# A second feed-forward by seven block products: one change to a two-layer diffusion step on one core

## The chip, the core and the metric

The kernel runs on one core of one Trainium2 chip, as one program. The metric is device time in microseconds (us). Before the change three runs took 1517.56 to 1518.67 us, median 1517.86. Besides these there is one execution recorded by the hardware profiler. A core has five engines that follow one instruction queue each and wait for each other by semaphores: TensorE (PE in the rows; PEld is its loading of weights), VectorE (DVE), ScalarE (ACT), GpSimd (POOL) and SyncE (SP), which here only starts DMA transfers. Matrix products are written to PSUM, everything else lives in SBUF.

## What is computed

The reference is one step of a two-layer network on 128 context tokens and 512 latent tokens of 1024 features. Each layer has a mixer and then a gated feed-forward with a convolution of three taps along the tokens; both are followed by a residual, a layer norm and a modulation by six vectors that come from a conditioning row c. What matters here is the feed-forward, with 2 x 2816 columns in `w_up`:

```python
def _conv_ffn(h, w_up, conv_w, conv_b, w_down):
    z = _dwconv(h @ w_up, conv_w, conv_b, 1, 1)
    g, v = z[..., :D_FF], z[..., D_FF:]
    return (jax.nn.silu(g) * v) @ w_down
...
        xp = _layernorm(ALPHA * xp + g2c * fp, ln2_g[l], ln2_b[l])
        xs = _layernorm(ALPHA * xs + g2s * fs, ln2_g[l], ln2_b[l])
```

The change touches it in layer 1, the second of the two. Everything is in float32.

## The kernel before

**Tokens.** Features lie on the 128 partitions and tokens along the columns: 128 context tokens, two columns of zeros, 512 latent tokens, T = 642 in all. `TOK` (line 26) has the five token tiles of 128.

**Products.** A float32 product is made of three passes of the format fp32r: each operand is split into a rounded part (hi) and what is left (lo), and `mm3` (line 152) adds hi x hi, hi x lo and lo x hi (lines 155, 156 and 157). `split` (line 97) makes the two parts: hi is a cast, mostly on ScalarE (line 99), lo a subtraction (line 102), of the activations on VectorE, of most weights on GpSimd.

**The feed-forward (`ffn`, line 534).** 2816 columns are 22 pairs of 128, each of a gate and a value. For one of the two, `ntile` makes 24 matmuls for the first 258 columns of tokens and 24 for the other 384, into one PSUM tile of 1024 columns (`A`, two of them). `conv` takes it from PSUM: ScalarE the middle tap with the bias (line 557), VectorE the outer taps (lines 558 and 559), ScalarE the Silu of the gate (line 561). `finish` multiplies the two (line 569, VectorE) and splits the product, which waits in the pool `s` for the down projection.

**The down projection.** It runs in parts (`PIECES`, line 28) of 4, 4, 4, 3, 3 and 4 pairs, and part q comes after the second pair of the part behind it. For a part and each of five token tiles there are two groups of matmuls of 512 columns, three to each pair, into a PSUM tile `B` (four of them). `accumulate` adds a group to `y` in SBUF (line 495 on VectorE; line 493 on ScalarE copies the first part's). The last part is added with the layer's gate and goes through the norm to the output.

**Weights.** SyncE's order of transfers is as written: `want` puts a weight tile in a queue, `load` starts its transfer into a raw buffer (`r`, four), `prep` splits it into the pool `w` (12 buffers of 4 KB per partition; a weight tile takes two). In layer 1 the value weight of the first pair and the odd down tiles have their lo made on VectorE, the others on GpSimd.

**Work beside it.** `back` is a list of generators, of which `tick` does one step at a time. In this stretch it holds `lazy` (line 439; the layer norm's factors and offsets applied to y on VectorE, lines 457 and 458) and `mod_vec` (line 257; the sixth modulation vector: VectorE multiplies rows of `wmT` by c, line 250, 16 instructions). c itself, after a Silu (line 1433), lies in the pool `v`, which has two buffers. Ahead of the last part comes `merge` (line 611), whose sums are on GpSimd (line 627).

**What sets the order.** SyncE's instructions stand as written. For the other engines a scheduler orders the instructions when the kernel is built, by when it reckons that they can begin; on the chip each engine then follows its row strictly. The transposes ahead of the first pair (`turn`, line 425, transposes on line 434 of what line 420 made) write the activations as hi and lo tiles of 2 x 642 columns.

## Time and profile before

| | |
|---|---|
| three runs, median | 1517.86 us |
| profiled execution, its own time | 1517.38 us |
| its span, first to last instruction | 1515.6 us |
| TensorE busy, matmuls | 1455.9 us (96%), 8768 |
| VectorE busy | 982.1 us (65%) |
| ScalarE busy | 599.9 us (40%) |
| GpSimd busy | 535.6 us (35%) |
| mean granted TensorE clock | 0.990 |

Shares are of the span. All rows are of the profiled execution; times in them count from the start of its span, and the 1.8 us between span and time lie around it. The shares are averages over stages with different limits, so the stretch that a change touches has to be read by itself: the second feed-forward goes from about 1030 us to the end. In a row, "<-" stands between what is written and what is read; a number in square brackets is how long the engine stood before the instruction, with the one that released it.

### The profile page before, as it was taken

Reading aid. Unit: us, or ns where it says so; the run is one execution under the profiler, and the core shown is the slowest. Engines: PE = TensorE matmul, PEld = TensorE weight load, DVE = VectorE, ACT = ScalarE, POOL = GpSimd, SP = SyncE. Lnnn points to the kernel's source line nnn. Section 1 sums busy time; section 2 is a strip of 40 time slices with the busy share of each in tenths; the row PEclk is TensorE's granted clock in tenths of the full one; section 3 lists DMA queues with packets and bytes.
Section 4 is the critical chain, followed back from the end, with each engine's and each line's share of the span. In section 5 each row is a group of like instructions: output and inputs, shape, how many; then the busy total and the mean of one; then the engine's idle time right before and its main releaser. Section 6 shows DMA issues by size and latency. Waiting matters only on the chain. (4 is left out here: it accounts for less than half of the span.)

```text
span 1515.6 us, 21970 instructions
## 1 busy us (share of the span) xinstructions
PE 1455.9 (96%) x8768; PEld 1311.8 (87%) x8768; DVE 982.1 (65%) x1498; ACT 599.9 (40%) x890; POOL 535.6 (35%) x431
## 2 busy tenths in 40 slices
PE   7989999999999999998999999999999999999997
PEld 5876879989898989888988888778999989898995
DVE  4685688456867697768699577767763424333558
ACT  3422354333132323235686656336333313132223
POOL 2241444333242425453462102853313232232343
PEclk9999999999999999999999999999999999999999
DMA  9544705344454445241321003433444222132231
GB/s 377 222 160 163 278 14 200 107 140 161 159 168 139 157 163 178 87 156 45 120 74 46 1 2 126 169 110 111 139 125 129 82 78 76 43 112 97 74 108 70
DMA packets 54757, 188.10 MB, mean 124 GB/s; under 512 B 6592, under 2 KB 7168, under 8 KB 54656
## 3 DMA queue, kind: packets, MB, share of 16 engines
q1 hardware_dynamic: 54656, 186.71, 36.4%
q8 instruction: 69, 1.13, 0.3%
q14 instruction: 32, 0.26, 0.1%
HBM read 175.96 MB, written 10.72 MB: 123 GB/s over the span
## 5 line engine op out<-in xcount | busy, mean ns | idle before, releaser
L102 POOL TENSOR_TENSOR w<-r,w 128x1024 fp32r<-128x1024 f32 (+2 forms) x130 | 326.3, 2520 | 679.7 <-ACT w L99 664.4
L155 PE MATMUL A<-s,w 128*128 128x258 f32 (+1 forms) x1672 | 524.1, 314 | 13.0 <-DVE t L559 5.9
L156 PE MATMUL A<-s,w 128*128 128x258 f32 (+1 forms) x1672 | 521.9, 312 | 0.5 <-DVE s L102 0.5
L157 PE MATMUL A<-s,w 128*128 128x258 f32 (+1 forms) x1672 | 521.2, 312 | 0.0
L155 PEld LDWEIGHTS A<-s,w 128*128 128x128 f32 x1672 | 317.5, 190 | 24.7 <-issue 14.2
L156 PEld LDWEIGHTS A<-s,w 128*128 128x128 f32 x1672 | 318.1, 190 | 4.3 <-issue 2.5
L99 ACT CAST w<-r 128x1024 fp32r<-128x1024 f32 (+2 forms) x181 | 183.8, 1033 | 345.3 <-PE B L156 136.3
L157 PEld LDWEIGHTS A<-s,w 128*128 128x128 f32 x1672 | 317.9, 190 | 2.5 <-issue 2.5
L155 PE MATMUL B<-w,s 128*128 128x512 f32 (+2 forms) x734 | 282.1, 386 | 3.4 <-DVE y L495 2.0
L156 PE MATMUL B<-w,s 128*128 128x512 f32 (+2 forms) x734 | 281.7, 384 | 2.9 <-DVE w L102 2.9
L157 PE MATMUL B<-w,s 128*128 128x512 f32 (+2 forms) x734 | 280.8, 384 | 0.9 <-DVE s L102 0.9
L558 DVE SCALAR_TENSOR_TENSOR t<-A,vec,t 128x641 f32<-128x641 f32 x88 | 77.7, 883 | 215.5 <-ACT t L557 215.5
L155 PEld LDWEIGHTS B<-w,s 128*128 128x128 f32 x734 | 137.7, 188 | 31.6 <-DVE y L495 2.2
L156 PEld LDWEIGHTS B<-w,s 128*128 128x128 f32 x734 | 137.8, 188 | 30.5 <-DVE w L102 3.7
L157 PEld LDWEIGHTS B<-w,s 128*128 128x128 f32 x734 | 138.0, 188 | 29.2 <-DVE s L102 1.4
L250 DVE SCALAR_TENSOR_TENSOR t<-r,v 128x1024 bf16<-128x1024 f32 x112 | 157.3, 1415 | 4.2 <-DMA r<-in_wmT_dram 3.2
L99 ACT CAST s<-t 128x642 fp32r<-128x642 f32 x60 | 43.8, 730 | 183.7 <-DVE t L569 148.8
L102 DVE TENSOR_TENSOR w<-r,w 128x1024 fp32r<-128x1024 f32 (+3 forms) x51 | 73.1, 1451 | 61.5 <-ACT w L99 61.4
L495 DVE TENSOR_TENSOR y<-B,y 128x512 f32<-128x512 f32 x80 | 54.7, 687 | 62.0 <-PE B L157 61.9
L557 ACT ACTIVATE t<-A,vec 128x642 f32<-128x642 f32 x88 | 77.7, 883 | 14.2 <-PE A L157 14.2
L559 DVE SCALAR_TENSOR_TENSOR t<-A,vec,t 128x641 f32<-128x641 f32 x88 | 77.8, 884 | 2.5
L561 ACT ACTIVATE t<-t 128x642 f32<-128x642 f32 x44 | 32.7, 742 | 99.7 <-DVE t L559 93.9
(259 smaller groups left out, 1596.8 us busy)
## 6 DMA issues: line engine op xcount, KB each, us to landing
r<-in_w_up_dram SPq DMA_DIRECT2D x88, 512.0 KB, 3.7
r<-in_wmT_dram SPq DMA_DIRECT2D x56, 512.0 KB, 3.3
r<-in_w_dn_dram SPq DMA_DIRECT2D x44, 512.0 KB, 4.0
s<-scr SPq DMA_DIRECT2D x20, 512.0 KB, 7.8
s<-in_wm_dram SPq DMA_DIRECT2D x16, 512.0 KB, 9.3
r<-in_wm_dram SPq DMA_DIRECT2D x16, 512.0 KB, 4.6
kept<-y SPq DMA_DIRECT2D x10, 512.0 KB, 3.5
r<-kept SPq DMA_DIRECT2D x10, 512.0 KB, 3.5
```

The source lines that it names most:

```text
L99: act.copy(hi, src)
L102: return lo_eng.tensor_tensor(lo, src, f(hi), ALU.subtract)
L155: pe.matmul(out, ah, bh, start=i == 0, stop=False)
L156: pe.matmul(out, ah, bl, start=False, stop=False)
L157: pe.matmul(out, al, bh, start=False, stop=i == n - 1)
L250: op = dve.scalar_tensor_tensor(junk, raw, 1.0, cb[s], ALU.mult, ALU.mult, accum_out=mc[l][:, m, s, k:k + 1])
L495: dve.tensor_tensor(acc[i][:, sl], ps, acc[i][:, sl], ALU.add)
L557: act.activation(t, z, AF.Identity, bias=cb, scale=w1)
L558: dve.scalar_tensor_tensor(t[:, 1:], z[:, :T - 1], w0, t[:, 1:], ALU.mult, ALU.add)
L559: dve.scalar_tensor_tensor(t[:, :T - 1], z[:, 1:], w2, t[:, :T - 1], ALU.mult, ALU.add)
L561: act.activation(t, t, AF.Silu)
```

## The change

The up projection of layer 1 is computed by blocks (`ffn_w`, which takes the place of `ffn(1, ...)`). The activations h are cut in halves of features (512 each) and halves of tokens (322 and 320 of the 642 columns, overlapping in two columns, so that every block has 322): A11, A12 by features for the first tokens, A21, A22 for the others. A pair's weights are four blocks of 512 x 128: B11 and B21 of the gate, B12 and B22 of the value. In place of the eight products of blocks there are seven, each of a block or a sum of blocks (Winograd's form of Strassen's scheme), and the four results are sums of the seven. Each product is 4 x 3 matmuls of 322 columns. The sums of activations S1 to S4 are made once, on VectorE, by `sums`, between the first pairs; while that goes on, the first `NPLAIN` = 2 pairs are computed as before. The sums of weights are made for each pair on GpSimd (four instructions of 512 columns, in `block`), each of the seven weight blocks is split with its lo on VectorE, and takes one buffer of the pool `w`; the lo of the down tiles is all on GpSimd. The results of the products are added on VectorE (`add`, seven instructions of 322 columns) into SBUF tiles zg and zv, from which the convolution now reads. `free` counts the weight buffers that are given back, and `pump_w` issues the next preparation when there is room among the 12.

The down projection goes in parts of three pairs (the last of four), each right after the pair that follows it. The norm's factor and offset rows lie in the pool `v` instead of `s`, and the rows of c for the sixth modulation are read by the generator `last_gate`, after the norm's rows.

The diff, cut to its core (after the change `split` stands at line 101, with the cast at line 103 and lo at line 106):

```diff
+PARTS = (0, 3, 6, 9, 12, 15, 18, 22)
+NPLAIN = 2
+TH = T // 2 + 1
+T2 = T - TH
...
+    def new_quads():
+        return [[[S([128, 4, TH], F32R) for _ in range(2)] for _ in range(2)] for _ in range(2)]
...
+            if self.quads:
+                cuts = ((c.start, min(c.stop, TH), 0), (max(c.start, T2), c.stop, 1))
+                for a, b, th in cuts:
+                    if a >= b:
+                        continue
+                    for kh in range(2):
+                        d = slice(a - th * T2, b - th * T2)
+                        split(hi[kh][th][:, :, d], lo[kh][th][:, :, d], p4[kh][:, :, a - c.start:b - c.start], act, dve)
+                return
...
-                    t = (S if n == 1 else Tm)([128, w])
+                    t = (Tm if n > 1 else V if self.l else S)([128, w])
...
+    def ffn_w(h):
...
+        ops = {"A11": (hi[0][0], lo[0][0]), "A12": (hi[1][0], lo[1][0]), "A22": (hi[1][1], lo[1][1])}
+        ORDER = ("A11", "S2", "S3", "A12", "S1", "A22", "S4")
...
+        def pump_w():
+            while tasks and live[0] + tasks[0][0] <= 12:
+                c, fn = tasks.pop(0)
+                live[0] += c
+                fn()
+        def free(n):
+            live[0] -= n
+            pump_w()
+        def block(p, j):
+            w = W([128, 2, 512], F32R)
+            wh, wl = w[:, 0, :], w[:, 1, :]
+            if j < 6:
+                g = raw(("g", p))
+                b11, b21 = g[:, :512], g[:, 512:]
+            v = raw(("v", p))
+            b12, b22 = v[:, :512], v[:, 512:]
+            src = b22 if j == 6 else (b11, b11, b12, b21, b12, b21)[j]
+            if j == 1:
+                pool.tensor_tensor(b12, b22, b12, ALU.subtract)
+                pool.tensor_tensor(b11, b12, b11, ALU.add)
+            elif j == 4:
+                pool.tensor_tensor(src, b22, b11, ALU.subtract)
+            elif j == 5:
+                pool.tensor_tensor(src, b21, b11, ALU.subtract)
+            split(wh, wl, src, act, dve)
+            ready_w[("u", p, j)] = w
+            if j == 5:
+                done(("g", p))
+            elif j == 6:
+                done(("v", p))
...
+        def plain(p):
+            r = raw(("d", p))
+            wh, wl = W([128, D], F32R), W([128, D], F32R)
+            split(wh, wl, r, act, pool)
...
+        def plan():
+            for p in range(NPLAIN, NP):
+                loads.append((("g", p), w_up[l, 2 * p]))
+                loads.append((("v", p), w_up[l, 2 * p + 1]))
+                for j in range(7):
+                    tasks.append((1, lambda p=p, j=j: block(p, j)))
+                if p in PARTS[1:]:
+                    q = PARTS.index(p) - 1
+                    yield q
+            yield NW - 1
+        for q in plan():
+            for d in range(PARTS[q], PARTS[q + 1]):
+                loads.append((("d", d), w_dn[l, d]))
+                tasks.append((2, lambda d=d: plain(d)))
...
+        def sums():
+            for n in ("S1", "S2", "S3", "S4"):
+                ops[n] = (S([128, 4, TH], F32R), S([128, 4, TH], F32R))
+            a11, a12, a21, a22 = ops["A11"], ops["A12"], (hi[0][1], lo[0][1]), ops["A22"]
+            for q in range(2):
+                ks = slice(2 * q, 2 * q + 2)
+                def part(pair):
+                    return f(pair[0][:, ks, :]), f(pair[1][:, ks, :])
+                def fin(n, src):
+                    split(ops[n][0][:, ks, :], ops[n][1][:, ks, :], src, act, dve)
+                def pair_op(x, y, op):
+                    t, e = Tm([128, 2, TH]), Tm([128, 2, TH])
+                    dve.tensor_tensor(t, x[0], y[0], op)
+                    dve.tensor_tensor(e, x[1], y[1], op)
+                    dve.tensor_tensor(t, t, e, ALU.add)
+                    return t
+                b11, b12, b21, b22 = (part(z) for z in (a11, a12, a21, a22))
+                s1 = pair_op(b21, b22, ALU.add)
+                fin("S1", s1)
+                yield
+                s2 = Tm([128, 2, TH])
+                dve.tensor_tensor(s2, s1, b11[0], ALU.subtract)
+                dve.tensor_tensor(s2, s2, b11[1], ALU.subtract)
+                fin("S2", s2)
+                yield
+                s4 = Tm([128, 2, TH])
+                dve.tensor_tensor(s4, b12[0], s2, ALU.subtract)
+                dve.tensor_tensor(s4, s4, b12[1], ALU.add)
+                fin("S4", s4)
+                yield
+                s3 = pair_op(b11, b21, ALU.subtract)
+                fin("S3", s3)
...
+        def up(p):
+            c1, c2, e = slice(0, TH), slice(TH, T), slice(TH - T2, TH)
+            p1, zg, zv = Tm([128, TH]), Tm([128, T]), Tm([128, T])
...
+            ps = A()
+            act.copy(p1, product(0, ps, 0))
+            free(1)
+            add(zv[:, c1], product(1, ps, 512), p1)
+            free(1)
+            ps = A()
+            add(zv[:, c2], product(2, ps, 0)[:, e], zv[:, e])
+            free(1)
+            add(zg[:, c1], product(3, ps, 512), p1)
+            free(1)
+            ps = A()
+            x5 = product(4, ps, 0)
+            add(zv[:, c1], x5, zv[:, c1])
+            free(1)
+            add(zg[:, c2], product(5, ps, 512)[:, e], zv[:, c2])
+            add(zv[:, c2], x5[:, e], zv[:, c2])
+            free(1)
+            tg = conv(zg, p, 0)
+            tick()
+            add(zv[:, c1], product(6, B(), 0), zv[:, c1])
+            free(1)
+            tv = conv(zv, p, 1)
+            tick(1 if p < NP - 2 else 3)
+            finish(p, tg, tv)
...
+        def rest(make_norm):
...
+            for p in range(1, NPLAIN):
+                up_plain(p)
+                free(4)
+            for _ in extra:
+                pass
...
+                up(p)
+                if p in PARTS:
+                    q = PARTS.index(p) - 1
+                    down(q)
...
-    nxt = nxt.rest(lambda: Norm(1, 0, (1, SA2)), sub(ffn, 1))
-    cb = [V([128, D]) for _ in range(2)]
-    for s in range(2):
-        sp.dma_start(cb[s], crow[s:s + 1].to_broadcast([128, D]))
-        act.activation(cb[s], cb[s], AF.Silu)
-    back.append(mod_vec(1, (5,), cb))
-    nxt.rest(lambda: Norm(1, 2, None), None)
+    nxt = nxt.rest(lambda: Norm(1, 0, (1, SA2)), sub(ffn_w))
+    def last_gate():
+        cb = [V([128, D]) for _ in range(2)]
+        for s in range(2):
+            sp.dma_start(cb[s], crow[s:s + 1].to_broadcast([128, D]))
+            act.activation(cb[s], cb[s], AF.Silu)
+        yield
+        yield from mod_vec(1, (5,), cb)
+    back.append(last_gate())
+    nxt.rest(lambda: Norm(1, 2))
```

**VectorE behind the second pair.** t and s are the temporaries and sums of `sums`, w weight buffers, y the rows that the norm is applied to. Before:

```order
L558 SCALAR_TENSOR_TENSOR t_9986<-A_9937,vec,t_9986 128x641
L457 TENSOR_TENSOR y_8735<-y_8735,s_9991 128x512
L559 SCALAR_TENSOR_TENSOR t_9986<-A_9937,vec,t_9986 128x641
L458 TENSOR_TENSOR y_8735<-y_8735,s_9993 128x512
L457 TENSOR_TENSOR y_8735<-y_8735,s_9991 128x512
L457 TENSOR_TENSOR y_8737<-y_8737,s_9991 128x512
```

After, from the same convolution on:

```order
L819 SCALAR_TENSOR_TENSOR t_9973<-A_9924,vec,t_9973 128x641
L785 TENSOR_TENSOR t_9986<-s_9399,s_9401 128x644
L820 SCALAR_TENSOR_TENSOR t_9973<-A_9924,vec,t_9973 128x641
L786 TENSOR_TENSOR t_9987<-s_9403,s_9405 128x644
L106 TENSOR_TENSOR w_10067<-r_9914,w_10067 128x512
L787 TENSOR_TENSOR t_9986<-t_9986,t_9987 128x644
L106 TENSOR_TENSOR w_10072<-r_9919,w_10072 128x512
L795 TENSOR_TENSOR t_9993<-t_9986,s_9398 128x644
L106 TENSOR_TENSOR s_9979<-t_9986,s_9978 128x644
L796 TENSOR_TENSOR t_9993<-t_9993,s_9402 128x644
L819 SCALAR_TENSOR_TENSOR t_10047<-A_9998,vec,t_10047 128x641
L106 TENSOR_TENSOR s_9981<-t_9993,s_9980 128x644
```

Between the instructions of two convolutions stand now the sums of halves (644 columns, lines 785 to 796), with their lo halves (s, line 106), where the norm's work (lines 457 and 458) stood, and lo halves of the coming blocks' weights (w, line 106); the norm's instructions stand further on.

**VectorE at the end of a down part.** y is what the parts are added to, B a group of matmuls. Before, at the end of the second part:

```order
L495 TENSOR_TENSOR y_10712<-B_11381,y_10712 128x512
L495 TENSOR_TENSOR y_10712<-B_11395,y_10712 128x512
L495 TENSOR_TENSOR y_10744<-B_11409,y_10744 128x512
L495 TENSOR_TENSOR y_10744<-B_11423,y_10744 128x512
L558 SCALAR_TENSOR_TENSOR t_11504<-A_11455,vec,t_11504 128x641
L559 SCALAR_TENSOR_TENSOR t_11504<-A_11455,vec,t_11504 128x641
```

After, at the end of the fourth part, up to the first sum of a product of the pair behind it (line 872):

```order
L514 TENSOR_TENSOR y_10496<-B_12203,y_10496 128x512
L514 TENSOR_TENSOR y_10524<-B_12214,y_10524 128x512
L106 TENSOR_TENSOR w_12236<-r_12005,w_12236 128x512
L106 TENSOR_TENSOR w_12241<-r_12116,w_12241 128x512
L514 TENSOR_TENSOR y_10524<-B_12225,y_10524 128x512
L106 TENSOR_TENSOR w_12244<-r_12116,w_12244 128x512
L106 TENSOR_TENSOR w_12249<-r_12239,w_12249 128x512
L106 TENSOR_TENSOR w_12252<-r_12116,w_12252 128x512
L106 TENSOR_TENSOR w_12255<-r_12239,w_12255 128x512
L106 TENSOR_TENSOR w_12276<-r_12116,w_12276 128x512
L872 TENSOR_TENSOR t_12261<-A_12262,t_12259 128x322
L106 TENSOR_TENSOR w_12295<-r_12239,w_12295 128x512
```

Where the next convolution followed the last groups, seven lo halves of weight blocks now stand ahead of the next pair's first sum.

**ScalarE and the rows of c.** v is the pool with two buffers. Before, in the odd layer's mixer ahead of the feed-forward:

```order
L389 ACTIVATE y_8735<-y_8735,m_9459,m_9464 128x512 x2
L1433 ACT_TABLE_LOAD
L1433 ACTIVATE v_9921<-v_9921 128x1024
L1433 ACTIVATE v_9922<-v_9922 128x1024
L370 ACTIVATE t_9510,m_9506<-y_8737,m_9505 128x1024
```

After, in the first part of the down projection:

```order
L512 COPY y_10524<-B_10525 128x512
L103 CAST w_10552<-r_10266 128x512
L103 CAST w_10557<-r_10379 128x512
L1750 ACTIVATE v_10437<-v_10437 128x1024
L512 COPY y_10524<-B_10536 128x512
L1750 ACTIVATE v_10438<-v_10438 128x1024
L875 COPY t_10575<-A_10578 128x322
L103 CAST w_10560<-r_10379 128x512
L103 CAST w_10565<-r_10555 128x512
```

The Silu of c moved from ahead of the feed-forward into its first down part, among the copies of that part's groups (line 512), the casts of weight blocks (line 103) and the copy of the next pair's first product (line 875).

## Rows read from the trace of the kernel before

**Rows 1.** Busy time by stretch (view of windows; columns are in the first line).

```profile
core 0: us, PE busy (x) PEld busy (x) DVE busy (x) ACT busy (x) POOL busy (x), PEclk, DMA share, GB/s
1051.19:1065.45 14.26, 14.26 (x96) 14.26 (x97) 10.24 (x11) 7.57 (x9) 6.72 (x3) 1.00 0.58 217
1030.00:1477.00 447.00, 442.83 (x2673) 417.47 (x2672) 213.48 (x274) 145.26 (x179) 135.69 (x65) 1.00 0.32 99
1036.86:1040.26 3.40, 3.40 (x19) 3.40 (x18) 3.40 (x7) 0.37 (x1) 0.76 (x2) 0.53 0.00 0
```

**Rows 2.** What TensorE waited for, 1030 to 1477 us: total, times, longest.

```profile
PE B L434 <- DVE t L420: 2.4, 1, 2.4
```

**Rows 3.** VectorE in order of time inside a down part: start, duration, what.

```profile
1220.24 0.69 DVE L495 TENSOR_TENSOR y<-B,y 128x512 f32<-128x512 f32 x1 [2.10 <-PE B L157]
1223.03 0.69 DVE L495 TENSOR_TENSOR y<-B,y 128x512 f32<-128x512 f32 x1 [2.10 <-PE B L157]
```

**Rows 4.** VectorE's groups, 1100 to 1300 us: total, mean ns, idle before.

```profile
L250 DVE SCALAR_TENSOR_TENSOR t<-r,v 128x1024 bf16<-128x1024 f32 x16 | 19.2, 1221 | 2.1 <-DMA r<-in_wmT_dram 1.9
L559 DVE SCALAR_TENSOR_TENSOR t<-A,vec,t 128x641 f32<-128x641 f32 x20 | 17.7, 886 | 0.7
...
L569 DVE TENSOR_TENSOR t<-t,t 128x642 f32<-128x642 f32 x11 | 9.1, 826 | 0.3
L495 DVE TENSOR_TENSOR y<-B,y 128x512 f32<-128x512 f32 x12 | 8.3, 690 | 17.4 <-PE B L157 17.4
...
L250 DVE DVE_READ_ACCUMULATOR t<-r,v 128x1 f32 x16 | 1.3, 82 | 0.0
```

**Rows 5.** VectorE in order of time, 1040 to 1115 us.

```profile
1054.24 2.49 DVE L569 TENSOR_TENSOR t<-t,t 128x642 f32<-128x642 f32 x1 [0.54 <-ACT t L561]
...
1066.20 1.28 DVE L457 TENSOR_TENSOR y<-y,s 128x512 f32<-128x512 f32 x2
1067.40 0.68 DVE L458 TENSOR_TENSOR y<-y,s 128x512 f32<-128x512 f32 x1
1068.00 0.88 DVE L558 SCALAR_TENSOR_TENSOR t<-A,vec,t 128x641 f32<-128x641 f32 x1
1068.80 2.10 DVE L458 TENSOR_TENSOR y<-y,s 128x512 f32<-128x512 f32 x1
```

**Rows 6.** TensorE in order of time, 1028 to 1066 us.

```profile
1029.77 0.66 PE L434 MATMUL B<-ident,t 128*128 128x128 f32 x4 [0.91 <-POOL t L420]
...
1030.63 0.29 PE L155 MATMUL A<-s,w 128*128 128x258 f32 x1
...
1036.45 0.66 PE L434 MATMUL B<-ident,t 128*128 128x128 f32 x4 [2.39 <-DVE t L420]
...
1038.12 0.42 PE L155 MATMUL A<-s,w 128*128 128x258 f32 x1
```

**Rows 7.** The buffers v from 1000 us: min/median/max ns, starts, shape.

```profile
L1433 ACT ACTIVATE v<-v x2: 1046/1054/1061, 1011.8 to 1012.7; 128x1024 f32<-128x1024 f32 x2
...
DMA to landing us min/median/max: 7.5/7.9/8.3
```

**Rows 8.** ScalarE's casts (line 99), 1030 to 1477 us, by shape.

```profile
L99 ACT CAST w<-r x63: 1030/1051/1057, 1044.4 to 1462.9; 128x1024 fp32r<-128x1024 f32 x63
...
L99 ACT CAST s<-t x21: 729/730/735, 1056.8 to 1469.1; 128x642 fp32r<-128x642 f32 x21
L99 ACT CAST s<-B x12: 350/373/415, 1033.2 to 1044.1; 128x256 fp32r<-128x256 f32 x12
```

**Rows 9.** GpSimd's sums of 512 columns (line 627), whole span.

```profile
L627 POOL TENSOR_TENSOR y<-y,r x20: 1287/1300/1824, 619.2 to 1467.1; 128x512 f32<-128x512 f32 x20
```

**Rows 10.** ScalarE's groups in a pair, 1030 to 1477 us.

```profile
L557 ACT ACTIVATE t<-A,vec 128x642 f32<-128x642 f32 x43 | 37.9, 882 | 3.4 <-PE A L157 3.4
...
L561 ACT ACTIVATE t<-t 128x642 f32<-128x642 f32 x22 | 16.3, 742 | 44.1 <-DVE t L559 44.1
```

**Rows 11.** GpSimd in order of time, about 1053 and 1066 us.

```profile
1053.65 2.40 POOL L102 TENSOR_TENSOR w<-r,w 128x1024 fp32r<-128x1024 f32 x1 [0.56 <-ACT w L99]
...
1066.61 3.73 POOL L102 TENSOR_TENSOR w<-r,w 128x1024 fp32r<-128x1024 f32 x1 [4.69 <-ACT w L99]
```

## What is expected, before the changed kernel was run

> **What bounds the kernel now.** I read the busy times of the stretch that the change touches, then what TensorE waited for in it, then the durations of the other engines' instructions there. In the second feed-forward (1030 to 1477 us) TensorE is busy 442.8 of 447 us, VectorE 213.5 (48%), ScalarE 145.3 and GpSimd 135.7 [rows 1]. Of the 4.2 us in which TensorE stood, 2.4 are one wait at the head of the stretch [rows 2]. So TensorE sets the pace, at full clock: the plain pair from 1051.19 to 1065.45 is 96 matmuls in 14.26 us [rows 1], 0.1485 each. What TensorE is spared is won, unless another engine now comes late. That engine is to be looked for.
>
> **What is saved.** Twenty pairs go from 96 matmuls (48 of 258 columns, 48 of 384, mean 321) to 84 of 322. No row has that width; it lies between the two, so I take 0.149 us: 12.52 a pair, 1.74 saved, 34.8 in all (1 us either way). The order has 240 rows fewer on TensorE, which is 20 x 12, so the change does what it says. The down projection keeps its 660 matmuls. Twelve of them come every 2.79 us [rows 3], so a group of nine takes 2.09 and a part of three (ten groups) 20.9. Against the profiled execution's 1517.4 us (the median of the runs is 0.5 above) that is 1482.6 if nothing waits.
>
> **VectorE's new load.** A pair had four conv instructions of 0.886, a product of 0.826, and a low half of the same width [rows 4], 5.2 us, and at times a weight's low half. All stay (two of the conv inputs now lie in SBUF), and seven low halves of 512 columns and seven sums of 322 from PSUM come on top. A 512-wide instruction on SBUF takes 0.68 alone and 0.60 when others follow (two in 1.28) [rows 5]. From PSUM 512 take 0.690 [rows 4]; less 190 columns at 1.1 ns (0.826 - 0.68 over 130 columns) gives 0.48 for 322, at least 0.43 (in proportion), at most 0.69. A pair is then 13.4 us (about 12 queued), beside 12.52 on TensorE; with a part of three, VectorE has 47 us in every 58.5. On the average that fits. But a pair's products pass through two PSUM tiles, so TensorE can't run more than a few products ahead of VectorE's sums, which stand in one queue with everything else. So I go through the places where that queue is late. A wait has a second price: after 0.91 us idle the matmuls ran on as before, after 2.39 a matmul of 258 columns took 0.42 [rows 6], and 3.4 us ran at a granted clock of 0.53 [rows 1], the lower level, which loses 1.6.
>
> **Term 1, the sums of halves: 20 us (10 to 28).** VectorE can't convolve pair 1's first half before 1051.2 + 7.1 + 0.9 = 1059.2. From there to the last half of S3 it has 39 instructions: 30 of 644 columns (0.74 queued, 0.83 alone), 4 conv, 5 low halves, 28.4 to 31.9 us; take 1090. TensorE ends pair 1 at 1065.4 and can do 39 of pair 2's 84 matmuls without that half; 45 remain, 6.7 us, so pair 2 ends at 1096.7 and not at 1077.9. With one slow clock 20. The low end is for sums that get ahead of the convs, the high one for GpSimd in the way.
>
> **Term 2, the sixth modulation: 22 us (8 to 32).** The Silus of its rows of c ran at 1011.8 us [rows 7]; now the rows need the two buffers that hold the norm's rows. During part 0 of the down projection VectorE has the rest of pair 3 and 17 of the 20 norm instructions, 16.5 us; only then do they leave, land after 7.9 and pass two Silus of 1.05. Six products of 1.3 [rows 4] stand ahead of pair 4's first sum: 34 us after the part began. TensorE has 20.9 + 48 x 0.149 = 28 until it needs that sum: 6. From there to pair 5's first sum VectorE has 7 sums, 12 low halves, 4 convs, 2 wide ones and 4 products, 21 us, TensorE 88 matmuls, 13.1: 8. Pair 5 loses 2 likewise, and 3 because its second raw weight is queued on SP behind those loads. Two slow clocks: 3.
>
> **Term 3, the pair after a part: 25 us (8 to 36).** Twelve weight buffers: six hold the part's weights, six the next pair's first blocks. The following blocks get theirs when the part's last group ends, and form one chain ahead of the next pair's first sum. A cast of 512 columns lies between 0.73 (642) and 0.373 (256) [rows 8]: 0.62. A GpSimd sum of 512 takes 1.30 [rows 9]. From the part's end: low half of block 0 at 0.8; GpSimd 2.1; casts of blocks 1 and 2 at 2.8 and 3.4; low half 4.1; GpSimd's block 4 at 5.4, another pair's 6.7, block 5 at 8.0; cast 8.7; low half 9.4; the sum 9.9. TensorE needs that sum after 42 matmuls, 6.3: 3.6 at least, 4.7 where VectorE and GpSimd shut each other out. 4.2 and a slow clock, 5.8, behind pairs 7, 10, 13 and 16, and 2 behind pair 19, whose sixth block stands after the sum.
>
> **Term 4, between pairs: 10 us (0 to 20).** The fourth block of the next pair but one takes the buffer of product 5. From that product's end: 0.2 + cast 0.62 + low half 0.68 + three sums 1.44 = 2.9 until a PSUM tile is free; TensorE has 10 matmuls, 1.5. That is 1.4, with 0.6 at the next two places, five times.
>
> Costed at nothing: ScalarE's added casts (7 x 0.62 and a copy against 2 x 1.05 a pair: 8.7 of 19.5 with the convs of 0.88 and Silu of 0.74 [rows 10]); the wider first group, which needs token tile 2's halves, 1.3 us later, and takes that from the 2.39 us wait behind it [rows 2]; the same bytes by DMA; the tail after 1477. Sum: 1482.6 + 77 = 1560.
>
> **The port.** GpSimd's low half at 1053.65 lasted to 1056.05; VectorE's product with two SBUF inputs, issued at 1054.24, took 2.49 and ended 0.68 after it. The GpSimd one at 1066.61 took 3.73 and ran only when VectorE came to an instruction that reads PSUM [rows 5, 11]. So one holds the other for a whole instruction. The Trainium skill ("SBUF — State Buffer", Who interferes with whom) states just that: a VectorE instruction with two SBUF inputs and a GpSimd one that reads SBUF take the shared pair in turn, and the second fully blocks. By that rule the trace agrees, and the rule speaks against a change that gives both engines more of this work; what it would make of the time is rival C.
>
> **Rivals.** A, faster: the scheduler's queue holds, the chains of terms 2 and 3 hide, only about 12 us of the sums and 6 between pairs stay: 1500. For it: on the average VectorE is 80% busy. Against it: 30 wide instructions have 8 us of cover. B, no change: the waits come to just 35 us (the sums and half of term 3): 1517. C, much slower: the port is the bound. In three pairs and a part GpSimd reads SBUF for 12 x 1.30 + 3 x 2.4 = 22.8 us and VectorE has two SBUF inputs for 21 x 0.68 + 12 x 0.886 + 6 x 0.826 = 29.9. If the sums from PSUM (21 x 0.48 + 10 x 0.69 = 17) find no GpSimd work to lie beside, that is 69.7 for three pairs where it was 3 x 14.26 + 20.9 = 63.7; with 20/3 such rounds 40, and terms 1 and, in part, 2: 1587. It decides once less than 11 of the 17 us overlap. Against it: in a part VectorE often waits for TensorE (2.10 us a group [rows 3]), and GpSimd can go then.
>
> **How the numbers follow.** The forecast (1521 to 1580, its own range 1535 to 1580) has 0.60, C 0.16, A 0.18, B 0.06. About 0.2% is what a measurement of this kernel can tell from no change, so faster 0.18, same 0.06, slower 0.76. The lows of the terms give 1509, the highs 1599; A reaches below. 1504 to 1598 leaves out 0.11 of A and 0.08 of C.
>
> **What will show it.** In the profile after: TensorE idle some 20 us between 1067 and 1090, ended by VectorE's low halves of S3 and S2; VectorE near 80% from 1090 on; 4 us of TensorE idle at the head of each pair after a part, ended by the first sum, with the clock down behind it; matmuls of 322 columns 0.149 apart. I am wrong if TensorE stays above 97% busy there (then A), or if VectorE's low halves take over 0.9 on the mean and rounds of three pairs 69 us (then C).

## The result and the profile after

Slower: 1599.43 us in the median (1597.66 to 1604.90) against 1518.26, a ratio of 1.0538 (95% interval 1.0510 to 1.0566). The direction was forecast, the size was not: 81 us were lost, 42 were forecast, and the time lies 1.4 us above the range. The profiled execution of the changed kernel took 1604.9 us; 7 us of what it has over before lie ahead of the second feed-forward, in work that stands in the same order as before, and are no part of the change. So the two are compared over the stretch from the last matmul of the mixer's projection to the last matmul of the feed-forward. Windows of before, columns as in [rows 1]:

```profile
1028.40:1505.20 476.80, 471.71 (x2798) 440.24 (x2796) 238.50 (x324) 157.19 (x197) 147.69 (x80) 1.00 0.30 96
```

The same stretch after, then three parts of it: up to the first down part; that part with pairs 4 to 6 and the next part; three pairs and a part further on.

```profile
1035.60:1591.40 555.80, 474.87 (x2558) 430.53 (x2555) 427.11 (x622) 213.13 (x325) 207.32 (x130) 0.92 0.25 84
1035.60:1129.00 93.40, 67.37 (x386) 63.93 (x384) 74.11 (x106) 42.71 (x64) 32.15 (x21) 0.82 0.18 57
1129.00:1241.60 112.60, 93.12 (x459) 81.96 (x458) 88.63 (x132) 38.86 (x62) 29.51 (x19) 0.88 0.37 126
1375.80:1443.70 67.90, 61.28 (x344) 55.85 (x343) 48.51 (x71) 25.33 (x39) 25.59 (x15) 0.97 0.22 70
```

The account: TensorE stands 80.9 us (555.8 - 474.9) where it stood 5.1, 75.8 more. It is busy 474.9 us where 471.7 - 34.8 = 436.9 were forecast, 38 more, at a mean granted clock of 0.92. Not all of the 38 us are clock. Summed over its busy time, the trace's granted clock lost 31.8 us against 1.7 before, 30 more. The other 8 lie at the edges of 33 waits: nothing overlaps the last matmul ahead of one, and the first behind one starts 0.25 us ahead of the next and not 0.15 (1386.18 below). So 75.8 + 30 + 8 - 34.8 = 79 us. What TensorE waited for after (in total, times, longest), which answers to [rows 2]:

```profile
PE A L866 <- DVE t L872: 43.0, 19, 5.6
PE B L866 <- ACT s L103: 17.0, 2, 9.2
PE B L866 <- ACT w L103: 7.4, 1, 7.4
PE A L866 <- ACT t L875: 3.8, 5, 1.2
```

The 17.0 us are the sums of halves of term 1, the 7.4 us a weight in pair 5 (term 2); the 43.0 us are PSUM tiles that VectorE's additions had not freed. In the later rounds three waits recur. The first two, behind a part, and the chain that the second ends, in order of time on all engines (start, duration):

```profile
1376.41 1.29 POOL L734 TENSOR_TENSOR r<-r,r 128x512 f32<-128x512 f32 x1 [19.43 <-DVE w L106]
...
1379.77 0.42 PE L866 MATMUL A<-s,w 128*128 128x322 f32 x1 [0.68 <-ACT t L875]
1379.83 1.61 POOL L736 TENSOR_TENSOR r<-r,r 128x512 f32<-128x512 f32 x1 [2.13 <-DVE w L106]
...
1381.39 1.29 POOL L733 TENSOR_TENSOR r<-r 128x512 f32<-128x512 f32 x1
...
1382.63 1.71 POOL L738 TENSOR_TENSOR r<-r 128x512 f32<-128x512 f32 x1
...
1384.38 1.66 ACT L103 CAST w<-r 128x512 fp32r<-128x512 f32 x3 [2.29 <-POOL r L738]
1385.03 0.69 DVE L106 TENSOR_TENSOR w<-r,w 128x512 fp32r<-128x512 f32 x1 [1.80 <-ACT w L103]
1385.64 0.49 DVE L872 TENSOR_TENSOR t<-A,t 128x322 f32<-128x322 f32 x1
...
1386.18 0.41 PE L866 MATMUL A<-s,w 128*128 128x322 f32 x1 [3.04 <-DVE t L872]
...
1386.43 0.31 PE L867 MATMUL A<-s,w 128*128 128x322 f32 x1
...
1386.58 0.32 PE L868 MATMUL A<-s,w 128*128 128x322 f32 x1
```

This is term 3's chain, another pair's sum (line 733) within it, and the forecast 9.9 us from the part's end to the first sum were 9.8 (1375.8 to 1385.6). The third wait, in the third pair:

```profile
1407.82 2.72 DVE L819 SCALAR_TENSOR_TENSOR t<-t,vec,t 128x641 f32<-128x641 f32 x2 [0.89 <-ACT t L818]
...
1408.30 1.56 POOL L733 TENSOR_TENSOR r<-r 128x512 f32<-128x512 f32 x1 [1.68 <-DMA r<-in_w_up_dram]
...
1409.81 2.96 POOL L106 TENSOR_TENSOR w<-r,w 128x1024 fp32r<-128x1024 f32 x1
...
1410.46 3.79 DVE L820 SCALAR_TENSOR_TENSOR t<-t,vec,t 128x641 f32<-128x641 f32 x2
...
1414.17 0.48 DVE L872 TENSOR_TENSOR t<-A,t 128x322 f32<-128x322 f32 x1
...
1414.71 0.42 PE L866 MATMUL A<-s,w 128*128 128x322 f32 x1 [2.81 <-DVE t L872]
```

Four conv instructions of 0.88 take 6.5 us, while GpSimd reads SBUF from 1408.30 to 1412.77; the addition that TensorE needs stands behind them, with no low half between. No term had this wait. VectorE's groups after (against 0.886 and 0.60 to 0.68 in [rows 4, 5]):

```profile
L106 DVE TENSOR_TENSOR w<-r,w 128x512 fp32r<-128x512 f32 x140 | 112.5, 824 | 41.7 <-ACT w L103 41.3
L819 DVE SCALAR_TENSOR_TENSOR t<-t,vec,t 128x641 f32<-128x641 f32 x40 | 45.4, 1154 | 6.9 <-ACT t L818 6.9
L820 DVE SCALAR_TENSOR_TENSOR t<-t,vec,t 128x641 f32<-128x641 f32 x40 | 44.7, 1137 | 0.1
...
L872 DVE TENSOR_TENSOR t<-A,t 128x322 f32<-128x322 f32 x60 | 29.2, 488 | 27.2 <-PE A L868 26.7
```

And behind 18 of the 30 waits of over half a us the matmuls run at the lower level for some time, which loses 1.8 us on the mean. TensorE, 1.3 us and then 4.7 us after the wait at 1414.71 (starts 0.27 us apart, then 0.15):

```profile
1416.02 0.47 PE L867 MATMUL A<-s,w 128*128 128x322 f32 x1
1416.29 0.47 PE L868 MATMUL A<-s,w 128*128 128x322 f32 x1
...
1419.46 0.31 PE L866 MATMUL A<-s,w 128*128 128x322 f32 x1
1419.61 0.31 PE L867 MATMUL A<-s,w 128*128 128x322 f32 x1
```

Behind the other 12 the full clock stays, so behind the 3.04 us at 1386.18. The wait at the same place one round earlier, 3.04 us too, lost 1.6.

### The profile page after: what moved, and what is told of

Its sections match the earlier page's. It is cut to its first block, busy times and chain, and to the rows that moved or that the text cites. A ratio compares the mean times of both kernels' runs of the same rounds, so it can differ in the third digit from the quotient of the medians.

```text
span 1603.1 us, 22134 instructions
## 1 busy us (share of the span) xinstructions
PE 1465.9 (91%) x8528; PEld 1308.8 (82%) x8528; DVE 1171.7 (73%) x1795; ACT 651.4 (41%) x1010; POOL 599.2 (37%) x480
## 5 line engine op out<-in xcount | busy, mean ns | idle before, releaser
L106 POOL TENSOR_TENSOR w<-r,w 128x1024 fp32r<-128x1024 f32 (+2 forms) x103 | 266.1, 2590 | 455.7 <-ACT w L103 369.7
L103 ACT CAST w<-r 128x512 fp32r<-128x512 f32 (+2 forms) x281 | 224.4, 823 | 392.0 <-PE B L160 110.2
L159 PE MATMUL A<-s,w 128*128 128x258 f32 (+3 forms) x1032 | 327.8, 318 | 17.5 <-DVE t L578 5.5
L160 PE MATMUL A<-s,w 128*128 128x258 f32 (+3 forms) x1032 | 326.3, 317 | 0.6 <-DVE s L106 0.6
L161 PE MATMUL A<-s,w 128*128 128x258 f32 (+3 forms) x1032 | 325.3, 316 | 0.0
L159 PEld LDWEIGHTS A<-s,w 128*128 128x128 f32 x1032 | 199.2, 193 | 28.5 <-issue 15.8
L106 DVE TENSOR_TENSOR w<-r,w 128x512 fp32r<-128x512 f32 (+3 forms) x178 | 167.1, 960 | 57.7 <-ACT w L103 57.2
L866 PE MATMUL A<-s,w 128*128 128x322 f32 x480 | 162.6, 343 | 47.3 <-DVE t L872 43.0
L160 PEld LDWEIGHTS A<-s,w 128*128 128x128 f32 x1032 | 199.7, 194 | 4.3 <-issue 2.5
L161 PEld LDWEIGHTS A<-s,w 128*128 128x128 f32 x1032 | 199.7, 194 | 2.5 <-issue 2.5
L867 PE MATMUL A<-s,w 128*128 128x322 f32 x480 | 158.2, 330 | 0.6 <-DVE s L106 0.6
L868 PE MATMUL A<-s,w 128*128 128x322 f32 x480 | 156.0, 328 | 0.0
L866 PEld LDWEIGHTS A<-s,w 128*128 128x128 f32 x480 | 99.0, 207 | 58.3 <-DVE t L872 47.3
L103 ACT CAST s<-t 128x642 fp32r<-128x642 f32 (+1 forms) x68 | 49.5, 729 | 165.1 <-DVE t L588 81.1
L577 DVE SCALAR_TENSOR_TENSOR t<-A,vec,t 128x641 f32<-128x641 f32 x44 | 38.9, 884 | 96.8 <-ACT t L576 96.7
```

Of the source, the lines that this page charges most:

```text
L103: act.copy(hi, src)
L106: return lo_eng.tensor_tensor(lo, src, f(hi), ALU.subtract)
L159: pe.matmul(out, ah, bh, start=i == 0, stop=False)
L160: pe.matmul(out, ah, bl, start=False, stop=False)
L161: pe.matmul(out, al, bh, start=False, stop=i == n - 1)
L577: dve.scalar_tensor_tensor(t[:, 1:], z[:, :T - 1], w0, t[:, 1:], ALU.mult, ALU.add)
```

## The experiments

Theory 1: TensorE is stopped at separate places, each with a mechanism of its own. Rival: VectorE's row is too long, whatever stands beside it. Times are medians; gains are against the changed kernel's 1599.4.

**One edit each.** The sums of halves left out:

```diff
-                ops[n] = (S([128, 4, TH], F32R), S([128, 4, TH], F32R))
+            ops["S1"], ops["S2"], ops["S3"], ops["S4"] = (hi[0][1], lo[0][1]), ops["A11"], ops["A12"], ops["A22"]
+            return
```

> Leaves out the sums S1 to S4 of the activations (30 wide instructions of 0.82 us and 8 casts); other quarters of the activations stand in their place, everything else is as in the changed kernel. Theory 1 (TensorE is stopped at four separate places, and at the first by these sums): the idle 18.4 us between 1070 and 1100 and the slow clock behind it go, 20 to 28 us less, 1572 to 1580, and nothing changes after 1150. Rival (VectorE is simply full): its queue is 25 us shorter and the gain is that, 25, but stands only if the later waits do not grow. If the stop was due to the weight blocks and not to the sums, under 10 us.

1575.6, 24 less, and the later rounds as they were: term 1 has the place and the price. Three plain pairs:

```diff
-NPLAIN = 2
+NPLAIN = 3
```

> Three plain pairs in place of two. Theory 1: the sums get another 14.3 us of cover, so most of the 18.4 idle us and half of the slow clock go; the third plain pair costs 1.9: 10 to 18 us less, 1582 to 1590. Rival (VectorE full): one pair less of sums and low halves, about 8 us of its work, 5 to 8 less. If the weight blocks were what TensorE waited for, no gain: they now come a pair later, too.

1583.4, 16 less: cover is what the sums lack. The rows of c early:

```diff
-    back.append(last_gate())
+    back.append(mod_vec(1, (5,), c_rows))
```

> The rows of c are loaded ahead of the feed-forward as before the change, and the norm's factor and offset instructions read these rows in place of their own (same instructions, other values; the norm's two row loads are left out). Theory 1: the chain norm, stores, c rows, modulation rows, next weight load (idle 5.6, 1.3, 1.8, 7.4, 1.3 and 2.1 us and slow clocks between 1151 and 1222) goes; what stays there is what other parts show behind them, about 4: 15 to 25 us less, 1575 to 1585. Rival (VectorE full): its work is the same to the instruction, so within 4 us of the changed kernel.

1591.0, 8 less, half of what was expected: the late load is not all of term 2; the 16 products still stand in VectorE's row. So they were moved out:

```diff
-    back.append(later(mod_vec(1, (0, 1, 2, 3, 4), cb), rg_consts()))
+    back.append(later(mod_vec(1, (0, 1, 2, 3, 4, 5), cb), rg_consts()))
-    back.append(last_gate())
```

> The sixth modulation vector is made with the other five of its layer, in the first layer's feed-forward and the mixer behind it, so the rows of c aren't read again and the 16 products leave the second feed-forward. Theory 1: of the idle 19.4 us between 1151 and 1222 only what other parts show behind them stays (3.7), with half of the slow clock: 16 to 24 us less, 1575 to 1583, and up to 5 us of it is given back where the products now stand. If, as the run with c's rows early suggests, only the late load counts, 8 us less, 1591, and the rest is the norm's instructions.

1590.0, 9 less. The stretch became 21.8 shorter, as expected (row below), but it begins at 1043.5 us, where the other single edits of the changed kernel had 1029 to 1031: the products cost some 12 us where they now stand, not up to 5 as expected.

```profile
1043.50:1577.50 534.00, 465.16 (x2556) 422.77 (x2554) 403.10 (x588) 210.84 (x322) 206.16 (x130) 0.94 0.24 77
```

The low halves of the down weights on VectorE:

```diff
-            split(wh, wl, r, act, pool)
+            split(wh, wl, r, act, dve)
```

> The low halves of all down projection weights (22 of 128x1024) go from GpSimd to VectorE. Theory 1 (the third wait of a round, 2.8 us and a slow clock, comes from VectorE and GpSimd shutting each other out of SBUF): lines 819 and 820 fall from 1.16 to under 0.95 on the mean, the low halves of 512 from 0.82 to about 0.70, and the third wait goes in the five rounds: 12 to 25 us less, 1575 to 1588, although VectorE gets 27 us more work. Rival (VectorE full): 10 to 27 us more, 1610 to 1626.

1587.5, 12 less, with 27 us more work on VectorE. Its groups and the wait that was 2.81:

```profile
L820 DVE SCALAR_TENSOR_TENSOR t<-t,vec,t 128x641 f32<-128x641 f32 x40 | 36.9, 952 | 0.1
L819 DVE SCALAR_TENSOR_TENSOR t<-t,vec,t 128x641 f32<-128x641 f32 x40 | 36.6, 942 | 2.1 <-ACT t L818 2.0
```

```profile
1332.59 0.41 PE L866 MATMUL A<-s,w 128*128 128x322 f32 x1 [0.86 <-DVE t L872]
```

More work and less time speak against the rival; the low halves of blocks stayed at 0.82. The additions given priority (the copy of the first product likewise):

```diff
-                dve.tensor_tensor(out, x, y, ALU.add)
+                with tc.high_priority():
+                    dve.tensor_tensor(out, x, y, ALU.add)
```

> The additions of products on VectorE and the copy of the first product on ScalarE are given priority when the engines' rows are ordered; nothing else is changed. If the wait of 3.0 us behind a part comes from the first addition standing behind low halves in VectorE's row, it falls by 1 to 2 us in the five rounds and the 0.7 us wait for the copy with it: 5 to 14 us less, 1585 to 1594. If the chain of weight buffers, GpSimd sums and casts decides, within 4 us of the changed kernel, since a block that isn't ready stops TensorE just as well.

1610.4, 11 more: a miss. The wait of 3.0 became two, of 1.5 and 1.2, and others were added (48 of over 0.3 us, 33 in the changed kernel). Parts of two:

```diff
-PARTS = (0, 3, 6, 9, 12, 15, 18, 22)
+PARTS = (0, 2, 4, 6, 8, 10, 12, 14, 16, 18, 22)
```

> Down projection in parts of two pairs (the last of four): a part then holds four of the twelve weight buffers, and all seven blocks of the next pair can be ready when it ends. Theory 1 (chain behind a part, from the shortage of buffers): the waits of 0.7 and 3.0 us behind a part fall under 1 in all, the part's end costs little, 10 to 20 us less, 1580 to 1590. Rival (each end of a part costs its 5 us, whatever its size): nine ends in place of six, 10 to 20 us more. Rival (VectorE full): three more parts are 30 more additions of 0.69 on VectorE, 20 us of it, up to 20 more.

1599.3, no change: a miss, but both waits are in it. TensorE in one round of two pairs:

```profile
1287.59 0.41 PE L866 MATMUL A<-s,w 128*128 128x322 f32 x1 [1.03 <-DVE t L872]
...
1303.71 0.42 PE L866 MATMUL A<-s,w 128*128 128x322 f32 x1 [2.48 <-DVE t L872]
...
1308.77 0.42 PE L866 MATMUL A<-s,w 128*128 128x322 f32 x1 [0.66 <-DVE t L872]
```

Behind a part 1.0 where it was 3.7, as the shortage of buffers asks; but the third wait now comes every two pairs. The next round, windows as above: 4.2 us idle and a granted clock of 1.00, so these waits carry no slow clock.

```profile
1311.50:1356.30 44.80, 40.60 (x231) 36.34 (x230) 35.59 (x51) 17.32 (x27) 16.86 (x10) 1.00 0.22 71
```

Parts of three in the kernel before:

```diff
-PIECES = (0, 4, 8, 12, 15, 18, 22)
+PIECES = (0, 3, 6, 9, 12, 15, 18, 22)
```

> The kernel before with parts of three pairs (each after the second pair behind it) and nothing else of the change. Theory 1: TensorE bound and VectorE half idle, so within 4 us of before, 1514 to 1522; then all of the loss belongs to the seven products and what they need. Rival: the smaller parts themselves cost (a sixth more additions, more switches), 5 us or more.

1524.7, 7 more, yet not from this stretch, which took 475.2 us (476.8 before) without a wait in its rounds: `PIECES` also sets the first layer's feed-forward, and the loss came ahead of the stretch. Smaller parts alone cost nothing here.

**What a wait costs.** The kernel before with pauses (8 and 0 copies; then 2 and 0; then 4 and 4):

```diff
+                if l == 1 and p in (3, 5, 7, 9, 11, 13, 15, 18, 19, 21):
+                    for _ in range((8, 0)[gv]):
+                        dve.tensor_copy(ps[:, 254:512], last_ps[0][:, 512:770])
```

> The kernel before, with ten pauses of TensorE in the second feed-forward: ahead of ten of its pairs VectorE copies 258 columns between PSUM tiles eight times, which TensorE has to wait for (about 3.5 us, estimated from 0.37 to 0.43 us a copy). The output is as before. It measures what a wait costs beyond its own length. If the prediction's price held (1.6 us of slow clock for a long wait): idle 35, slow clock 16, total 45 to 55 over before. If the price in the changed kernel's accounts is right (40 us of slow clock to 76 of idle, one half): idle 35, slow 18 to 25. If a wait costs its length alone: 35.

> The same ten pauses with two copies each, about 1 us. If short waits carry no slow clock (as the 0.91 us wait of before seemed to show): 10 us over before, all of it idle. If they carry it as well: 10 idle and 10 to 18 slow.

> The long pause in two halves: four copies ahead of the gate's matmuls and four ahead of the value's, 7 us later, on the same ten pairs. The idle sum is that of the long pauses or a little more. If the slow clock goes by the sum of idle time: the same total as the long pauses within 5 us. If it goes by the number of waits: up to 16 us more, which is what giving the additions priority suggests (one wait of 3.0 became two of 1.5 and 1.2 and the total grew). If waits of 2 us carry none: 15 less.

1571.9, 1551.4 and 1605.5. The pauses did not come out ten and equal, since matmuls of other groups moved into some of them and weights came late in others (one pause was 10.0 us), so the totals of the last two missed (32 and 86 over before). The 52 of the first lie in the branch of the prediction's own price. The stretch of each, in this order of runs, a fence each:

```profile
1030.60:1559.00 528.40, 484.59 (x2797) 448.48 (x2795) 273.10 (x401) 157.18 (x196) 152.71 (x78) 0.96 0.27 86
```

```profile
1032.00:1534.70 502.70, 478.36 (x2798) 443.71 (x2796) 244.86 (x339) 156.17 (x196) 148.50 (x77) 0.98 0.28 91
```

```profile
1029.20:1590.80 561.60, 494.09 (x2798) 451.87 (x2796) 274.04 (x402) 157.32 (x197) 151.00 (x78) 0.94 0.25 81
```

Against before's 471.7 busy and 5.1 idle: 12.9 us more busy on 38.7 more idle, 6.7 on 19.2, 22.4 on 62.4, a third each time. By the traces' granted clock 11.1, 4.9 and 17.6 of these are the lower level. Wait by wait it does not follow the length: in the first run 10.0 us idle lost 2.9 us to it, 8.5 and 8.6 lost 2.5 and 2.3, 3.2 lost 1.7, and waits of 1.25, 1.44 and 2.39 lost none. The split pauses did not come out as halves (the copies ended five waits, weights and the sixth modulation most others), so what cutting a pause does is not shown.

**GpSimd.** All together (three plain pairs, low halves on VectorE, parts of two behind the first, sixth vector early):

> The changed kernel with three plain pairs, all low halves of down weights on VectorE, parts of two pairs behind the first (the last of four), and the sixth modulation vector made with the other five. By the single runs (16, 12, 0 and 9 us) 1562; since the parts of two took the wait behind a part away and brought the third wait of a round more often, and that wait goes with the low halves, 10 to 15 less: 1547 to 1552. It stays above before. If VectorE is full after all (its low halves and three more parts' additions are 47 us more work): no better than the best single run, 1583 or more.

1565.5, 34 less: close to the 37 of the single gains, but the further 10 to 15 that were expected did not come. Then GpSimd's four sums of weight blocks left out of `block`, alone, with the down weights' low halves on VectorE, and from the version with all edits:

```diff
-            if j == 1:
-                pool.tensor_tensor(b12, b22, b12, ALU.subtract)
-                pool.tensor_tensor(b11, b12, b11, ALU.add)
-            elif j == 4:
-                pool.tensor_tensor(src, b22, b11, ALU.subtract)
-            elif j == 5:
-                pool.tensor_tensor(src, b21, b11, ALU.subtract)
```

> The changed kernel without GpSimd's four sums of weight blocks in each pair (the raw blocks stand in their place). That takes the chain behind a part away and most of what GpSimd reads beside VectorE in a pair; VectorE's instructions are the same. If the chain and the shared port make the waits: idle behind a part 3.7 to under 1 in five rounds, less in pairs 4 to 6 as well, with the slow clock behind these waits 25 to 40 less: 1560 to 1575. If VectorE's row is too long by itself: within 10 of the changed kernel.

> The same, with the down weights' low halves on VectorE, so that GpSimd has no work beside the pairs. Chain and port: the third wait of a round goes as well, VectorE's convolutions fall to 0.88 and its low halves of 512 to 0.65; 10 to 15 less than without the sums alone, 1545 to 1562. VectorE too full: its 27 us more of work show, and the time is that of the run without the sums or more.

> The run with four edits together, without GpSimd's sums of weight blocks. This is the floor of the scheme as built, without chain and port: what is left is VectorE's own row, which was busy 86% in the rounds of that run. If chain and port made the rest of the waits: 20 to 35 less than the 1565, 1530 to 1545, and TensorE idle under 3% in the rounds. If VectorE is the bound now: within 10 of 1565.

1548.3, 1530.0 and 1510.6: 51, 69 and 89 less, each 12 to 19 below the range that was expected, and VectorE's instructions are the same as in the kernel that each was cut from, or more. The last is the only version of `ffn_w` below the kernel before (0.9948 of it), but it leaves out sums that the result needs. VectorE's groups without GpSimd's sums, then without its low halves as well:

```profile
L106 DVE TENSOR_TENSOR w<-r,w 128x512 fp32r<-128x512 f32 x140 | 93.3, 691 | 11.2 <-ACT w L103 10.7
L812 DVE SCALAR_TENSOR_TENSOR t<-t,vec,t 128x641 f32<-128x641 f32 x40 | 44.6, 1133 | 5.7 <-ACT t L811 5.4
```

```profile
L106 DVE TENSOR_TENSOR w<-r,w 128x512 fp32r<-128x512 f32 x140 | 92.7, 689 | 8.7 <-ACT w L103 8.4
L812 DVE SCALAR_TENSOR_TENSOR t<-t,vec,t 128x641 f32<-128x641 f32 x40 | 34.7, 882 | 0.7 <-ACT t L811 0.5
```

The low halves fall with the first, the convolutions with the second. To part the chain from the reading, GpSimd did its sums into a tile that nobody reads:

```diff
-                pool.tensor_tensor(src, b22, b11, ALU.subtract)
+                pool.tensor_tensor(spare, b22, b11, ALU.subtract)
```

> The changed kernel in which GpSimd still does its four sums of weight blocks in each pair, from the same raw weights, but into a spare tile, and the weight blocks are cast from the raw weights: the same reading of SBUF beside VectorE, but no chain. (The spare tile is of 16 bits for want of room, and the products are of other blocks than they should be.) If the chain makes the 51 us that the run without the sums gained: 1545 to 1560. If the shared port makes them: 1585 to 1605. In between, the parts are read from it directly.

1597.2, as slow as with the chain: GpSimd's reading without the chain is enough to make this time. The chain is gone (behind a part 0.8 where it was 3.7), but GpSimd, which waits for little but the raw weights now, does its work in one piece beside the convolutions, and the third wait grew to 4.1:

```profile
1401.89 1.31 POOL L734 TENSOR_TENSOR spare<-r 128x512 bf16<-128x512 f32 x1
...
1403.97 3.12 DVE L820 SCALAR_TENSOR_TENSOR t<-t,vec,t 128x641 f32<-128x641 f32 x2 [0.89 <-ACT t L819]
...
1407.02 4.80 DVE L821 SCALAR_TENSOR_TENSOR t<-t,vec,t 128x641 f32<-128x641 f32 x2
...
1412.27 0.64 PE L867 MATMUL A<-s,w 128*128 128x322 f32 x1 [4.12 <-DVE t L873]
```

So it doesn't show that the chain cost nothing, only that taking it away gains nothing while GpSimd reads. Last, the whole computation, all edits together but with the sums on VectorE and the down weights' low halves back on GpSimd; and a version of it with seven plain pairs and c early:

```diff
-                pool.tensor_tensor(src, b22, b11, ALU.subtract)
+                dve.tensor_tensor(src, b22, b11, ALU.subtract)
...
-NPLAIN = 3
+NPLAIN = 7
```

> The run with four edits together (1565), in which VectorE makes the four sums of weight blocks and GpSimd the low halves of the down weights: the chain has no other engine in it and a sum takes 0.68 us in place of 1.3, while VectorE has 52 us more and 27 us less to do. If chain and port weigh more than VectorE's load: 1540 to 1558. If VectorE, busy 86% in those rounds, is full by then: 1570 or more.

> A version built on what the runs showed, with the whole computation: the weight block sums on VectorE (as in the 1534 run), parts of two pairs, seven plain pairs ahead of fifteen by seven products, so that the norm's instructions, then the 16 products of the sixth modulation (rows of c loaded early, as before the change), then the sums of halves each have two plain pairs of VectorE's free time to themselves. Of the 1534 run's loss some 35 us stood at its start and 11 in moving the modulation ahead; its later rounds gained 5.5 us in four pairs. Theory (GpSimd beside VectorE was the loss, and VectorE has room if its extra work is spread): 15 pairs gain 1.4 each, 20 in all, and the start costs 0 to 12 more than before: 1498 to 1512, faster than before by 0.4 to 1.3%. Rival (VectorE too full in the start as well): 1518 to 1530.

1534.1, 6 below the expected range and the best of the whole computation by `ffn_w` (1.0105 of before, 1.0086 to 1.0124), and 1567.2, a miss. Stretch and four pairs with two parts of the first:

```profile
1041.80:1521.00 479.20, 451.88 (x2569) 412.50 (x2566) 430.07 (x670) 209.12 (x315) 85.64 (x51) 0.98 0.26 86
...
1303.10:1382.70 79.60, 78.70 (x458) 72.36 (x457) 71.70 (x117) 34.20 (x52) 9.58 (x4) 1.00 0.25 80
```

Before, four pairs and 120 matmuls of down projection (2.79 us for twelve, [rows 3]) took 4 x 14.26 + 27.9 = 84.9, so these rounds gain 5.3, with VectorE 90% busy. Waits at the start and the end of the stretch and the moved products give it back. What stopped TensorE in the version with seven plain pairs:

```profile
PE A L159 <- ACT w L103: 20.5, 2, 12.7
...
PE B L222 <- DVE m L217: 9.3, 1, 9.3
```

The weights of plain pairs, loaded only when they are taken, stood behind the modulation's loads: an order of loads that this edit made. Its later rounds took 79.6 us, too. No version with the whole computation ran faster than before.

## Why the prediction was wrong

- **What bounds and what is saved.** Right: 240 matmuls are gone, and at full clock 322 columns start 0.148 us apart.
- **The waits.** Terms 1 to 3 stand where they were forecast: idle 26.0 us up to the first part (18.8 forecast for the sums, besides before's 5.1 at the head; 18.4 of it are ended by the sums), 19.5 in pairs 4 to 6 (19 forecast), 18.6 behind the later parts (18.8 forecast). The sums are 28 wide instructions, not 30. Term 4's 10 us came out by luck: in the later rounds no block's chain stops TensorE between pairs, but the third wait, which no term had, takes 11.3 us in four rounds. In all 75.8 us against 66.6.
- **The step that failed: how many waits carry a slow clock.** The price of 1.6 us was near, but it was counted seven times: 1.6 in term 1, 3 in term 2, four times 1.6 in term 3, 11 in all. The lower level followed 18 waits and took 30 us more than before. That is 19 of the 37 us by which the stretch missed the forecast; 9 are idle time, and 8 are the edges of the waits, a term put at nothing. Up to the first part it is 8.0 where 1.6 were counted, in pairs 4 to 6 9.1 where 3 were, behind the later parts 6.3 where 6.4 were, and behind the third wait and in the last pair 6.8 where none was.
- **The port was a rival and not a term.** The forecast took VectorE's durations from rows where GpSimd was quiet, and priced the chain behind a part by its length. Without GpSimd's sums, and then without its low halves too, 51 and 69 us of the 81 go; with the reading and no chain only 2 do. Rival C had this mechanism, at 0.16 and 1587, in a form that was half right: rounds of three pairs and a part took 67.9 to 70.2 us where it said 69.7, but by waits, with VectorE 71% busy (48.5 of 67.9), and its low halves took 0.82, not 0.9. The Trainium skill ("SBUF — State Buffer", Who interferes with whom) says that a VectorE instruction with two SBUF inputs contends with a GpSimd one that reads SBUF; the 3.79 us for two convolutions beside 2.96 us of GpSimd, and 0.88 each without it, agree.
- **Rival A** fell with the 80.9 us. The parts of three, costed at nothing, cost nothing.

Open: why one wait is followed by the lower level and another of the same length is not; and how much the chain would cost without the port.

## What to carry to other kernels

When an edit gives work to VectorE and GpSimd at once, price it by rows where both read SBUF, not by an engine's load: here VectorE was 71% busy and still late. With GpSimd's sums moved to it, and the down weights' low halves back to GpSimd, the kernel was 31 us faster, though VectorE was then 90% busy in the rounds. Where TensorE will wait, count the waits and not only their sum: a wait cost a quarter of a us at its edges, and one that the lower level followed cost 1.8 us more on the mean. The saved matmuls paid in rounds without such collisions; what is done once for a stretch has to be earned back by its rounds, and here it was not.

## What the runs showed of the hardware

- Idle time of TensorE can be followed by matmuls at the lower of its two levels: 322 columns start 0.27 us apart in place of 0.15 (1416.02 and after). In the changed kernel 18 of 30 waits of over half a us were followed by it, and of two waits of 3.04 us at the same place in their rounds one was and one was not. In the version with all edits 4 of 38 were: 8.3 us lost on 53 us idle, against 31.8 on 80.9.
- Two VectorE conv instructions (two SBUF inputs, 641 columns) took 4.80 us beside a row of GpSimd instructions, 1.76 alone (two of 0.882); GpSimd's sums of 512 took 1.76 each in that row, 1.29 at 1376.41 in the changed kernel.
